# Gate columns from the raw input in plain fp32, 32 columns wide, on four column strips

## The chip, the cores and the metric

The kernel runs on one core of one Trainium2 chip. The metric is device time in microseconds (us). The kernel before takes 1498.56 us, the median of three runs (1497.97 to 1499.13).

## What is computed

One layer of a hybrid streaming trunk for 320 tokens (256 of a new stream, 64 of a running one), model width 2048. The part that matters here is the combined input projection, of whose columns the last 16 are the "gate columns" (8 for beta, 8 for the decay of the gated DeltaNet heads):

```python
h = rmsnorm(x, g_pre_mix)                  # x * rsqrt(mean(x*x) + eps) * g
p = h @ w_in
...
q, k, v, z, b_raw, a_raw = ...             # b_raw, a_raw: the 16 gate columns
beta = jax.nn.sigmoid(b_raw)
g = -jnp.exp(a_log) * jax.nn.softplus(a_raw + dt_bias)
o, s = gated_delta_chunked(q, k, v, hchunks(g), hchunks(beta), s0)
```

After it come a Conformer convolution over half of the mix width, the output projection, and a convolutional feed-forward network with the large w_up and w_down.

## The kernel before

Everything is held transposed: features on the 128 partitions, the 320 tokens along the free axis, so the width of 2048 is 16 k-blocks (KB). The row factor of RMSNorm (`rb`, a 128 x 320 tile that holds the same row of 320 numbers on every partition) is applied after the products, since it is one number for each token; the norm weight g1 is multiplied into the activations.

**Products.** Large products run in fp32r on values split in two: `whi` is the weight rounded by a ScalarE cast (L214), `wlo` the rest by a VectorE subtraction (L215), and the activations are split likewise (`hi_t`, `lo_t`, called hh and hl in the profile). Each 128 x 128 block of weights takes three matmuls of 128 x 320 (hi·hi L230, hi·lo L231, lo·hi L234). A projection block of 128 columns is 48 of them. Raw weights, `whi` and `wlo` have three buffers each; a projection block uses two (h1, h2: eight k-blocks each), so a cast waits for the matmuls that read the third-last `whi`.

**The order of the work.** The stream of these "dense" matmuls is written out block by block, and each is counted by `tick`. At every 20th tick the jobs that are due (generators: the norm, the gates, the stages of the DeltaNet, convolution taps) are advanced: their next piece of code is put behind the dense matmul that has just been issued, at a raised priority. Where a small job stands in each engine's queue thus hangs on the tick count.

**The start.** The first 192 matmuls make four blocks at once (`ps_first`, two z blocks, a q block and a k block) while the input arrives. Then come the gate columns, `gate_products` (L303): 32 dense matmuls from `hi_t` and `lo_t`, whose stationary operand `wbz` is 128 wide with the cast of the gate weights in columns 0 to 15, their rest in columns 16 to 31 and zeros beyond. They accumulate in the bank `psba`, of which 32 partitions are used. Then comes the block FIRST_V (number 48 of the projection, a v block), then block 25 and block 17 (k and q blocks), all in `psq` banks. The pool `ps_p` has two banks: psba, block 48, block 25 (in psba's bank) and block 17 (in block 48's) take them in turn, so block 17's first matmul waits until block 48's sum has been read, by `qb<-psq` (L623).

**The norm** is a job: `rstd` (six matmuls of one column, L256), then `rr` (DVE L261, POOL L262), and, 36 ticks later, `psb` (three transposes, L269) and `rb<-psb` (ACT L402). Behind `rb` wait, on VectorE, the two z tiles (L949), the q and k tiles `qb<-ps_first` (L623), the gates' `baT` (L424, L425) and the short convolution `cq` (L629, whose first tap is ACT L627), and then `qb<-psq`.

**The gates** are a job: `baT<-psba` (ACT L421, L422; 32 partitions), times `rb` (DVE L424, L425), three transposes of 32 x 128 (`pst_ba`, L430), a copy and an addition that sums the two halves (L432, L433), and small functions.

**The DeltaNet** runs pair by pair of heads in jobs beside the later projection blocks. Three places are named below: `px` (PE L789) waits for `zh` (ACT L784) in the inversion of small triangular blocks; `pvns` (PE L884) waits for `rhs` (DVE L876); and `pvn` (PE L855) for `rh` (DVE L896). Other VectorE work stands between these: the base inversion of the next pair (L745 to L759, 40 partitions), weight splits and convolution taps (L560).

Of the kernel before, what the change touches and what calls it, by code (L numbers as in the profile page):

```python
# [9 lines left out]
F32 = mybir.dt.float32  # L10
# [7 lines left out]
P = 128  # L18
D = 2048
KB = D // P  # L20
# [80 lines left out]
def trunk_kernel(ctx, tc, ins, outs):  # L101
# [46 lines left out]
    def tick(mm):  # L148
        dense[0] = mm.ins
        dense[1] += 1  # L150
        if dense[1] % GAP == 0:
            g, t0, behind, due = 0, held_t[0], dense[0], []
            t = t0
            n0 = len(nc.cur_bb.bb.instructions)
            for job in sorted(jobs, key=lambda j: j[0]):
                if job[0] <= dense[1] and g + job[2] <= 4 and t + job[3] <= 2:
                    g += job[2]
                    t += job[3]
                    due.append(job)
            for job in due:  # L160
                if not job[4]:
                    behind = advance(job, behind)
            scalar = newest(mybir.EngineType.Activation, n0)
            for job in due:
                if "scale" in job[4]:
                    with ExitStack() as e:
                        if scalar is not None:
                            e.enter_context(tc.issue_after(scalar))
                        advance(job)
            held_t[0] = t - t0  # L170
            front = newest(mybir.EngineType.DVE, n0)
            for _ in range(min(pace[0], len(taps))):
                next_tap(front)
# [21 lines left out]
    def cv(name, n=P, m=P):  # L195
        o, _ = CST[name]
        return cst[0:n, o:o + m] if o < NCST1 else cst2[0:n, o - NCST1:o - NCST1 + m]
# [106 lines left out]
    def gate_products(wz):  # L304
        psba = ps_p.tile([P, 512], F32, tag="p", name="psba")
        for k in range(KB):
            tick(PE.matmul(psba[:, 0:T], wz[:, k, :], hi_t[k], start=(k == 0), stop=False))
            tick(PE.matmul(psba[:, 0:T], wz[:, k, :], lo_t[k], start=False, stop=(k == KB - 1)))
        return psba


# [1 line left out]
    with tc.tile_pool(name="xp", bufs=1) as xp:  # L313
        xt = [xp.tile([P, 4, T], F32, tag=f"x{i}", name=f"xt{i}") for i in range(4)]
        wg = []

        def load_x(k0, k1):
            nc.sync.dma_start(xt[k0 // 4][:, k0 % 4:k0 % 4 + k1 - k0, :], ins["x"][:, k0:k1, :])

        def load_first(k0, k1):  # L320
            nc.sync.dma_start(wg[-1][:, (k0 % 2) * FW:(k0 % 2 + k1 - k0) * FW], ins["w_first"][:, k0 * FW:k1 * FW])

        with tc.high_priority():
            nc.scalar.dma_start(par[:, 0:NGV], ins["par"][:, 0:NGV])
            for k in range(0, KB, 2):
                wg.append(wst.tile([P, HALF], F32, tag="w", name="w"))
                for kk in ((k, k + 1), (k + 1, k + 2)) if k < 4 else ((k, k + 2),):
                    load_x(*kk)
                    load_first(*kk)
            nc.sync.dma_start(cst, ins["cst"][:, 0:NCST1])  # L330
            wba = xp.tile([P, KB, 16], F32, tag="wba", name="wba")
            nc.sync.dma_start(wba, ins["w_ba"])
        wbz = xp.tile([P, KB, P], F32R, tag="wbz", name="wbz")
        G.memset(wbz.bitcast(F32), 0.0)
        nc.sync.dma_start(par[:, NGV:NPAR], ins["par"][:, NGV:NPAR])
        nc.sync.dma_start(gpar[:, 0:8], ins["a_log"].partition_broadcast(P))
        nc.sync.dma_start(gpar[:, 8:16], ins["dt_bias"].partition_broadcast(P))
        psw = ps_g.tile([P, 512], F32, tag="g", name="psw")
        with tc.high_priority(offset=PRI_E):
            keep_warm(psw, NWARM)  # L340

            last = {}

            def then(eng, fn, *args, **kw):
                with ExitStack() as e:
                    if eng in last:
                        e.enter_context(tc.issue_after(last[eng].ins))
                    last[eng] = fn(*args, **kw)

            def split_part(hi, lo, w, o, n):  # L350
                then(S, S.copy, hi[:, o:o + n], w[:, o:o + n])
                then(V, V.tensor_tensor, lo[:, o:o + n], w[:, o:o + n], hi[:, o:o + n].bitcast(F32), ALU.subtract)

            ssum = xp.tile([P, 2, T], F32, tag="ssum", name="ssum")

            def squares(k):
                x = xt[k // 4][:, k % 4:k % 4 + 2, :]
                if k == 0:
                    then(S, S.activation, ssum, x, AF.Square)
                else:  # L360
                    sq = xp.tile([P, 2, T], F32, tag="sq", bufs=2, name="sq")
                    then(S, S.activation, sq, x, AF.Square)
                    then(V, V.tensor_tensor, ssum, ssum, sq, ALU.add)

            for k in range(KB):
                x = xt[k // 4][:, k % 4, :]
                g = pv("g1", k)
                then(S, S.activation, hi_t[k], x, AF.Identity, scale=g)
                then(V, V.scalar_tensor_tensor, lo_t[k], x, g, hi_t[k].bitcast(F32), ALU.mult, ALU.subtract)
                if k % 2 == 0:  # L370
                    pre.append((wsp.tile([P, HALF], F32R, tag="whi", name="whi"), wsp.tile([P, HALF], F32R, tag="wlo", name="wlo")))
                if k < 4:
                    split_part(*pre[-1], wg[k // 2], (k % 2) * FW, FW)
                elif k % 2:
                    split_part(*pre[-1], wg[k // 2], 0, 2 * FW)
                if k % 2 and k >= 5:
                    squares(k - 5)
            then(S, S.copy, wbz[:, :, 0:16], wba)
            then(V, V.tensor_tensor, wbz[:, :, 16:32], wba, wbz[:, :, 0:16].bitcast(F32), ALU.subtract)
            for k in (KB - 4, KB - 2):  # L380
                squares(k)
        for i, b in enumerate(FIRST):
            pool = (ps_t, ps_g)[i // 2]
            ready[b] = pool.tile([P, 512], F32, tag=pool.name[-1], name="ps_first")
        for k0 in range(0, KB, 2):
            hi, lo = pre[k0 // 2]
            for ks in ((k0,), (k0 + 1,)) if k0 < 4 else ((k0, k0 + 1),):
                for wt in (hi, lo):
                    for k in ks:
                        for i, b in enumerate(FIRST):  # L390
                            ps = ready[b][:, 0:T]
                            o = (k - k0) * FW + i * P
                            w = wt[:, o:o + P]
                            xh, xl = hx(k)
                            tick(PE.matmul(ps, w, xh, start=(k == 0 and wt is hi), stop=(k == KB - 1 and wt is lo)))  # L395
                            if wt is hi:
                                tick(PE.matmul(ps, w, xl, start=False, stop=False))

        def first_norm():
            rr, _ = rstd([ssum[:, 0, :], ssum[:, 1, :]])  # L400
            yield 36, 1, 0
            S.copy(rb, rstd_rows(rr)[0])  # L402

        job = start(first_norm(), 24, 1)
        psba = gate_products(wbz)
        ready[FIRST_V] = in_block(FIRST_V, "psq")
        finish(job)
# [5 lines left out]


    gate = {}
    cst2 = act.tile([P, NCST - NCST1], F32, tag="bl7", name="cst2")
    nc.sync.dma_start(cst2, ins["cst"][:, NCST1:NCST])

    def gates():
        baT = cb.tile([32, 3, P], F32, tag="un", bufs=1, name="baT").rearrange("p c f -> p (c f)")  # L420
        S.copy(baT[:, 0:T], psba[0:32, 0:T])  # L421
        S.copy(baT[:, T:T + TS], psba[0:32, TP:T])  # L422
        yield 1, 0, 0
        V.tensor_tensor(baT[:, 0:T], baT[:, 0:T], rb[0:32, :], ALU.mult)  # L424
        V.tensor_tensor(baT[:, T:T + TS], baT[:, T:T + TS], rb[0:32, TP:T], ALU.mult)  # L425
        ba = const.tile([P, 3, 16], F32, tag="ba", name="ba")
        yield LAG_WAIT, 0, 1
        pst = ps_t.tile([P, 512], F32, tag="t", name="pst_ba")
        for c in range(3):
            PE.transpose(pst[:, c * 32:(c + 1) * 32], baT[:, c * P:(c + 1) * P], cv("ident", 32, 32))  # L430
        ps3 = pst[:, 0:96].rearrange("p (c f) -> p c f", c=3)
        S.copy(ba, ps3[:, :, 0:16])  # L432
        V.tensor_tensor(ba, ba, ps3[:, :, 16:32], ALU.add)  # L433
        beta = const.tile([P, 3, NH], F32, tag="beta", name="beta")
        S.activation(beta, ba[:, :, 0:8], AF.Tanh, scale=0.5)
        G.tensor_scalar(beta, beta, 0.5, 0.5, ALU.mult, ALU.add)
# [878 lines left out]
```

## Time and profile before

| what | value |
|---|---|
| median of three runs | 1498.56 us (1497.97 to 1499.13) |
| the profiled execution's span, first to last instruction | 1497.8 us |
| mean granted TensorE clock in it | 0.997 |
| DVE busy | 996.1 us (67%) |
| ACT busy | 727.9 us (49%) |
| POOL busy | 229.2 us (15%) |
| DMA over the span | 149 GB/s |

The median stands 0.76 us above the span of the profiled execution; this covers what lies before the first and after the last instruction. PE is TensorE's matmuls, PEld its weight loads, DVE is VectorE, ACT ScalarE, POOL GpSimd, SP the engine that issues the DMAs. A busy time of the profile counts matmuls that overlap once. In a row of the timeline the columns are the start, the duration, the engine, the line, the operation and its tiles with their shapes, how many instructions the row holds, and in square brackets the idle time of that engine just before it and the instruction that ended it.

### The profile page before, as it was taken

Reading aid. Unit: us, or ns where it says so; the run is one execution under the profiler, and the core shown is the slowest. Engines: PE = TensorE matmul, PEld = TensorE weight load, DVE = VectorE, ACT = ScalarE, POOL = GpSimd, SP = SyncE. Lnnn points to the kernel's source line nnn. Section 1 sums busy time; section 2 is a strip of 40 time slices with the busy share of each in tenths; the row PEclk is TensorE's granted clock in tenths of the full one; section 3 lists DMA queues with packets and bytes.
Section 4 is the critical chain, followed back from the end, with each engine's and each line's share of the span. In section 5 each row is a group of like instructions: output and inputs, shape, how many; then the busy total and the mean of one; then the engine's idle time right before and its main releaser. Section 6 shows DMA issues by size and latency. Waiting matters only on the chain.

```text
span 1497.8 us, 27263 instructions
## 1 busy us (share of the span) xinstructions
PE 1481.6 (99%) x10609; PEld 1460.4 (98%) x10610; DVE 996.1 (67%) x1816; ACT 727.9 (49%) x1329; POOL 229.2 (15%) x390
## 2 busy tenths in 40 slices
PE   9999999999999999999999999999999999999998
PEld 8999999989999999999999999999999999999997
DVE  6779886978989678766345666445666545666554
ACT  7764556554544565544434444334444333444453
POOL 0111101120010000332002222002223101222101
PEclk9999999999999999999999999999999999999999
DMA  8435453544434744444554444455444455444453
GB/s 289 142 128 157 141 155 120 146 139 134 130 106 142 221 151 141 148 149 128 149 169 151 151 154 134 140 156 164 154 152 141 136 146 173 153 146 152 130 152 118
DMA packets 98281, 224.22 MB, mean 150 GB/s; under 512 B 18792, under 2 KB 39528, under 8 KB 98152
## 3 DMA queue, kind: packets, MB, share of 16 engines
q1 hardware_dynamic: 98008, 222.45, 47.7%
q8 instruction: 83, 1.36, 0.4%
q14 instruction: 46, 0.38, 0.1%
q10 hardware_dynamic: 144, 0.03, 0.0%
HBM read 215.33 MB, written 7.12 MB: 149 GB/s over the span
## 4 chain that ended last, share of the span: by engine, by line
PE 86%; DVE 6%; ACT 3%; DMA 2%; issue 2%; POOL 1%; SPq 0%; ACTq 0%; DVEq 0%
PE psu L234 13%; PE psu L231 13%; PE psu L230 13%; PE psdn L230 7%; PE psdn L231 6%; PE psdn L234 6%; PE psq L234 2%; PE psq L230 2%; PE psq L231 2%; PE psm L231 2%; PE psm L230 2%; PE psm L234 2%; DVE wlo L215 1%; PE psu L1108 1%; PE ps_first L395 1%
## 5 line engine op out<-in xcount | busy, mean ns | idle before, releaser
L214 ACT CAST whi<-w 128x1024 fp32r<-128x1024 f32 (+2 forms) x440 | 412.6, 940 | 481.7 <-PE psu L231 169.0
L215 DVE TENSOR_TENSOR wlo<-w,whi 128x1024 fp32r<-128x1024 f32 (+2 forms) x440 | 477.0, 1085 | 199.0 <-ACT whi L214 127.8
L230 PE MATMUL psu<-hi,whi 128*128 128x320 f32 x1344 | 397.0, 309 | 0.0
L231 PE MATMUL psu<-lo,whi 128*128 128x320 f32 x1344 | 397.0, 309 | 0.0
L230 PEld LDWEIGHTS psu<-hi,whi 128*128 128x128 f32 x1344 | 252.3, 188 | 0.0
L231 PEld LDWEIGHTS psu<-lo,whi 128*128 128x128 f32 x1344 | 252.3, 188 | 0.0
L234 PE MATMUL psu<-hi,wlo 128*128 128x320 f32 x1344 | 224.4, 309 | 0.0
L234 PEld LDWEIGHTS psu<-hi,wlo 128*128 128x128 f32 x1344 | 204.0, 188 | 0.0
L231 PE MATMUL psdn<-gl,whi 128*128 128x320 f32 x660 | 195.9, 310 | 0.0
L1141 POOL COPY nffn<-fbuf 128x2 f32<-128x2 f32 x88 | 101.5, 1153 | 586.9 <-DVE fbuf L1139 583.7
L1139 DVE TENSOR_TENSOR fbuf<-psu,rb 128x256 f32<-128x256 f32 x88 | 37.3, 424 | 168.9 <-PE psu L234 168.9
L230 PE MATMUL psdn<-gh,whi 128*128 128x320 f32 x480 | 142.8, 309 | 0.0
L231 PEld LDWEIGHTS psdn<-gl,whi 128*128 128x128 f32 x660 | 123.9, 188 | 0.3
L230 PE MATMUL psq<-hh,whi 128*128 128x320 f32 x352 | 106.2, 315 | 0.0
L231 PE MATMUL psq<-hl,whi 128*128 128x320 f32 x352 | 104.1, 309 | 0.0
L230 PEld LDWEIGHTS psdn<-gh,whi 128*128 128x128 f32 x480 | 90.1, 188 | 0.0
L234 PE MATMUL psdn<-gh,wlo 128*128 128x320 f32 x480 | 89.9, 309 | 0.0
L234 PEld LDWEIGHTS psdn<-gh,wlo 128*128 128x128 f32 x480 | 75.3, 188 | 0.0
L230 PEld LDWEIGHTS psq<-hh,whi 128*128 128x128 f32 x352 | 66.1, 188 | 0.3
L231 PEld LDWEIGHTS psq<-hl,whi 128*128 128x128 f32 x352 | 66.1, 188 | 0.2
L560 DVE SCALAR_TENSOR_TENSOR cvt<-ub,par,cvt 128x320 f32<-128x320 f32 x120 | 65.2, 543 | 0.2
L1184 DVE TENSOR_TENSOR y<-y,psdn 128x320 f32<-128x320 f32 x45 | 22.0, 488 | 59.1 <-PE psdn L234 59.1
(356 smaller groups left out, 2483.3 us busy)
## 6 DMA issues: line engine op xcount, KB each, us to landing
w<-in_w_up SPq DMA_DIRECT2D x176, 512.0 KB, 3.6
w<-in_w_in SPq DMA_DIRECT2D x88, 512.0 KB, 3.9
w<-in_w_down SPq DMA_DIRECT2D x64, 384.0 KB, 3.1
w<-in_w_down SPq DMA_DIRECT2D x64, 320.0 KB, 3.0
w<-in_w_out SPq DMA_DIRECT2D x32, 320.0 KB, 3.8
w<-in_w_out SPq DMA_DIRECT2D x16, 384.0 KB, 3.2
w<-in_w_first SPq DMA_DIRECT2D x6, 512.0 KB, 6.9
wtp<-wsp SPq DMA_DIRECT2D x4, 640.0 KB, 6.0
```

What stands on the lines that cost most here:

```text
L214: S.copy(hi[:, 0:width], w[:, 0:width])
L215: V.tensor_tensor(lo[:, 0:width], w[:, 0:width], hi[:, 0:width].bitcast(F32), ALU.subtract)
L230: tick(PE.matmul(ps, wh, xh, start=(first and k0 + j == 0), stop=False))
L231: tick(PE.matmul(ps, wh, xl, start=False, stop=False))
L234: tick(PE.matmul(ps, lo[:, j * P:(j + 1) * P], xh, start=False, stop=(final and k0 + j == nk - 1)))
L395: tick(PE.matmul(ps, w, xh, start=(k == 0 and wt is hi), stop=(k == KB - 1 and wt is lo)))
L560: return lambda: V.scalar_tensor_tensor(acc, x, w, acc, ALU.mult, ALU.add)
L1108: PE.matmul(pss[i][:, 0:T], wt[:, o:o + P], x, start=(k == 0 and n == 0), stop=(k == KB - 1 and n == 2))
L1139: V.tensor_tensor(buf[:, 2:258], psu[:, 0:TP], rb2[:, 0:TP], ALU.mult)
L1141: G.tensor_copy(nffn[:, b, 0, :], buf[:, 256:258])
L1184: V.tensor_tensor(y[:, n, :], y[:, n, :], psd[:, 0:T], ALU.add)
```

## The change

The gate columns are multiplied in plain fp32 from the raw input `xt`, 16 products of 128 x 32 (stationary) by 128 x 320 (moving). Product k writes the 32 output partitions from 32·(k mod 4), so that four products in a row use four different strips of 32 columns of the array, and psba holds four partial sums. The norm weight is multiplied into the 16 gate columns instead (DVE), `wbz` is 32 wide and its ScalarE cast goes; the memset that clears it covers 512 elements of a partition instead of 2048. The products are counted by 16 ticks, all behind the last one, where there were 32.

Behind them `baT` has 128 partitions instead of 32, and the three transposes become three plain fp32 products with `pick` (128 x 16: ones where partition mod 32 equals the column, made from the identity by a VectorE reduction), which sum the four strips and turn them at once. The addition of the two halves goes.

```diff
     def gate_products(wz):
         psba = ps_p.tile([P, 512], F32, tag="p", name="psba")
         for k in range(KB):
-            tick(PE.matmul(psba[:, 0:T], wz[:, k, :], hi_t[k], start=(k == 0), stop=False))
-            tick(PE.matmul(psba[:, 0:T], wz[:, k, :], lo_t[k], start=False, stop=(k == KB - 1)))
+            i = 32 * (k % 4)
+            mm = PE.matmul(psba[i:i + 32, 0:T], wz[:, k, :], xt[k // 4][:, k % 4, :], start=(k < 4), stop=(k >= KB - 4),
+                           skip_group_check=True)
+        for _ in range(16):
+            tick(mm)
         return psba
...
-        wbz = xp.tile([P, KB, P], F32R, tag="wbz", name="wbz")
-        G.memset(wbz.bitcast(F32), 0.0)
+        wbz = xp.tile([P, KB, 32], F32, tag="wbz", name="wbz")
+        G.memset(wbz, 0.0)
...
-            then(S, S.copy, wbz[:, :, 0:16], wba)
-            then(V, V.tensor_tensor, wbz[:, :, 16:32], wba, wbz[:, :, 0:16].bitcast(F32), ALU.subtract)
+            then(V, V.tensor_tensor, wbz[:, :, 0:16], wba, pv("g1").unsqueeze(2).to_broadcast((P, KB, 16)), ALU.mult)
...
+    pick = const.tile([P, 16], F32, tag="pick", name="pick")
...
     def gates():
-        baT = cb.tile([32, 3, P], F32, tag="un", bufs=1, name="baT").rearrange("p c f -> p (c f)")
-        S.copy(baT[:, 0:T], psba[0:32, 0:T])
-        S.copy(baT[:, T:T + TS], psba[0:32, TP:T])
+        baT = cb.tile([P, 3, P], F32, tag="un", bufs=1, name="baT").rearrange("p c f -> p (c f)")
+        S.copy(baT[:, 0:T], psba[:, 0:T])
+        S.copy(baT[:, T:T + TS], psba[:, TP:T])
+        V.tensor_reduce(pick, cv("ident").rearrange("p (a j) -> p j a", j=32)[:, 0:16, :], AX.X, ALU.add)
         yield 1, 0, 0
-        V.tensor_tensor(baT[:, 0:T], baT[:, 0:T], rb[0:32, :], ALU.mult)
-        V.tensor_tensor(baT[:, T:T + TS], baT[:, T:T + TS], rb[0:32, TP:T], ALU.mult)
+        V.tensor_tensor(baT[:, 0:T], baT[:, 0:T], rb, ALU.mult)
+        V.tensor_tensor(baT[:, T:T + TS], baT[:, T:T + TS], rb[:, TP:T], ALU.mult)
         ba = const.tile([P, 3, 16], F32, tag="ba", name="ba")
         yield LAG_WAIT, 0, 1
         pst = ps_t.tile([P, 512], F32, tag="t", name="pst_ba")
         for c in range(3):
-            PE.transpose(pst[:, c * 32:(c + 1) * 32], baT[:, c * P:(c + 1) * P], cv("ident", 32, 32))
-        ps3 = pst[:, 0:96].rearrange("p (c f) -> p c f", c=3)
-        S.copy(ba, ps3[:, :, 0:16])
-        V.tensor_tensor(ba, ba, ps3[:, :, 16:32], ALU.add)
+            PE.matmul(pst[:, c * 16:(c + 1) * 16], baT[:, c * P:(c + 1) * P], pick, start=True, stop=True)
+        S.copy(ba, pst[:, 0:48].rearrange("p (c f) -> p c f", c=3))
```

The lines of the changed program are numbered two to four higher than before. With 16 ticks fewer, the ticks at which jobs come due fall on other matmuls of the weight stream, and where a job's instructions stand on each engine shifts with them.

At the start of the program, on ScalarE, around the copy of `rb` from `psb`, there stood before (baT holds the gate columns, strict is a constant, whi is a weight cast, zT a z tile):

```order
L422 COPY baT<-psba 32x64
L471 CAST strict<-cst 128x128
L214 CAST whi<-w 128x1024
L402 COPY rb<-psb 128x320
L214 CAST whi<-w 128x1024
L950 ACT_TABLE_LOAD
L950 ACTIVATE zT_615<-zT_615 128x320
```

And now:

```order
L425 COPY baT<-psba 128x64
L473 CAST strict<-cst 128x128
L214 CAST whi<-w 128x1024 x3
L404 COPY rb<-psb 128x320
L952 ACT_TABLE_LOAD
L952 ACTIVATE zT_599<-zT_599 128x320
```

The casts ahead of the copy were those of block 25's second half; now those of block 17's two halves stand there too. On PE, `psb` stood behind 36 matmuls of `psq` (after all 32 gate products) and stands behind 64 now, while block 17 begins behind 96 in both.

On VectorE, around the two `rhs` of the third pair of heads (tmp, dn and wi are the base inversion of the pair after it, cvt and odd convolution taps, wlo a weight split, rh what pvn waits for, sg a gate tile of the convolution), there stood before:

```order
L752 TENSOR_TENSOR tmp<-dn,wi 40x512
L560 SCALAR_TENSOR_TENSOR odd<-ub_587,par,odd 128x320
L754 TENSOR_REDUCE dn<-tmp 40x64
L876 SCALAR_TENSOR_TENSOR rhs<-ks,neG,vh 64x128
L756 TENSOR_TENSOR tmp<-wi,dn 40x512
L533 TENSOR_TENSOR sg<-psgate,rb 128x320
L876 SCALAR_TENSOR_TENSOR rhs<-ks,neG,vh 64x128
```

And now:

```order
L878 SCALAR_TENSOR_TENSOR rhs<-ks,neG,vh 64x128
L747 TENSOR_TENSOR tmp<-wi,dn 40x72
L562 SCALAR_TENSOR_TENSOR cvt<-ub_571,par,cvt 128x320
L749 TENSOR_REDUCE wi<-tmp 40x2x6
L878 SCALAR_TENSOR_TENSOR rhs<-ks,neG,vh 64x128
L747 TENSOR_TENSOR tmp<-wi,dn 40x98
L239 TENSOR_TENSOR bl_4407<-af,bh_4406 128x320
L749 TENSOR_REDUCE wi<-tmp 40x2x7
L562 SCALAR_TENSOR_TENSOR odd<-ub_571,par,odd 128x320
L535 TENSOR_TENSOR sg<-psgate,rb 128x320
L754 TENSOR_TENSOR tmp<-dn,wi 40x512
L215 TENSOR_TENSOR wlo<-w,whi 128x1024
```

The wide steps of the base inversion (40x512) stood ahead of the two `rhs` and between them; now they stand behind both and ahead of `rh` (L898).

## The prediction

> **What bounds the kernel now.** I read the page first: the busy times, then the chain that ended last, with its shares by engine.
>
> ```profile
> PE 1481.6 (99%) x10609; PEld 1460.4 (98%) x10610; DVE 996.1 (67%) x1816; ACT 727.9 (49%) x1329; POOL 229.2 (15%) x390
> PE 86%; DVE 6%; ACT 3%; DMA 2%; issue 2%; POOL 1%; SPq 0%; ACTq 0%; DVEq 0%
> ```
>
> TensorE is busy for 1481.6 of 1497.8 us. So a matmul taken out shortens the kernel by its time, unless PE then waits; only some 16 us of waits exist. Next, the timeline of PE where it waits beside the DeltaNet, and the table of windows around two of these waits (in each engine's column the busy time; PEclk is the granted clock).
>
> ```profile
> 158.08 0.46 PE L789 MATMUL px<-wtp,zh 32*16 32x16 f32 x38 [0.97 <-ACT zh L784]
> 315.46 0.48 PE L789 MATMUL px<-wtp,zh 32*16 32x16 f32 x38 [1.95 <-ACT zh L784]
> 352.18 0.46 PE L884 MATMUL pvns<-rhs,wtp 128*128 128x128 f32 x2 [1.86 <-DVE rhs L876]
> core 0: us, PE busy (x) PEld busy (x) DVE busy (x) ACT busy (x) POOL busy (x), PEclk, DMA share, GB/s
> 312.00:316.00 4.00, 2.05 (x64) 1.78 (x65) 3.66 (x5) 2.97 (x8) 0.00 (x0) 0.94 0.58 198
> 316.00:320.00 4.00, 4.00 (x44) 3.96 (x39) 2.47 (x13) 1.35 (x6) 0.02 (x1) 0.63 0.45 137
> 350.00:354.00 4.00, 2.14 (x13) 1.98 (x13) 3.94 (x7) 2.61 (x10) 0.00 (x0) 0.89 0.08 10
> 354.00:358.00 4.00, 4.00 (x24) 4.00 (x23) 3.49 (x7) 1.23 (x3) 0.00 (x0) 0.69 0.58 145
> 159.00:163.00 4.00, 4.00 (x26) 3.87 (x27) 1.48 (x5) 3.43 (x11) 1.18 (x7) 1.00 0.31 105
> ```
>
> The waits of 1.95 and 1.86 us were each followed by a stretch at a lowered clock. From 312 to 320 the missing clock is 4·0.06 + 4·0.37 = 1.7 us of PE time, from 350 to 358 it is 4·0.11 + 4·0.31 = 1.7 us. After the wait of 0.97 us (the row 159 to 163) the clock stayed at 1.00. So a wait of PE near 2 us cost 1.7 us more than itself in both cases here.
>
> **The gate products.** PE's timeline has the first of them, its neighbours, the column sums of the norm that run among them, and the first matmul of block 48.
>
> ```profile
> 33.91 0.31 PE L307 MATMUL psba<-hh,wbz 128*128 128x320 f32 x1
> 38.02 1.40 PE L256 MATMUL pst<-cst,ssum 128*128 128x1 f32 x12
> 39.28 0.39 PE L307 MATMUL psba<-hh,wbz 128*128 128x320 f32 x1
> 39.96 0.31 PE L230 MATMUL psq<-hh,whi 128*128 128x320 f32 x1
> ```
>
> From 33.91 to 38.02 stand 28 products: 0.147 us each, 4.7 us for 32. The column sums took 1.26 us of PE (38.02 to 39.28), and stay. For a plain fp32 product of 128 x 128 by 128 x 320 the trace has the end of the program, which turns the output with one; for strips it has the small triangular blocks.
>
> ```profile
> 1487.13 2.33 PE L1230 MATMUL fin<-y,cst 128*128 128x320 f32 x8
> 1489.30 0.70 PE L1151 MATMUL fin<-x,cst 128*128 128x320 f32 x2
> 166.27 0.31 PE L231 MATMUL psz<-hl,whi 128*128 128x320 f32 x1
> 166.51 0.50 PE L806 MATMUL pz<-wtp,np 32*32 32x32 f32 x20
> 166.94 0.42 PE L230 MATMUL psz<-hh,whi 128*128 128x320 f32 x1
> 170.41 0.32 PE L815 MATMUL py<-zq,wtp 32*32 32x32 f32 x5
> ```
>
> The group of L806's records has their durations (least, median and most, in ns):
>
> ```profile
> L806 PEld LDWEIGHTS pz<-wtp,np x80: 101/108/108, 166.5 to 395.4; 32*32 32x32 f32 x80
> L806 PE MATMUL pz<-wtp,np x80: 191/191/212, 166.5 to 395.4; 32*32 32x32 f32 x80
> ```
>
> Eight records took 2.17 us, 0.271 each, and a plain fp32 product leaves two records (L806's ten products leave 20): 0.54 us a product, 8.7 us for 16 in series. So in plain fp32 the gates cost more, not less, unless the strips run beside each other. That they can: the L806 records, on two strips in turn, follow each other by (0.50 − 0.19)/19 = 16 ns, where those of L815, on one, take (0.32 − 0.19)/4 = 32 ns (0.19 us is one record's median). With four strips beside each other 16 products take four rounds of 0.54 us, 2.17 us, and going in and out of narrow tiles costs some 0.3 us (166.27 to 166.94 is 0.67 us for L806: less one dense product, 0.15, and 20 records of 16 ns, 0.2 are left, and the wider last record is still running). I take **G = 2.45 us** for the gates; the bound above is 8.7 (no overlap), the bound below 2.2. Saved on PE: 4.7 − 2.45 = 2.25 us.
>
> [...] In the trace L815 and its neighbour L813 share rows and interleave, but only with 32 rows; the case of 128 rows is in no row here. [...]
>
> **What waits next.** The products are not followed by a stream that is always ready: block 17 needs the bank of block 48, which VectorE frees behind `rb`. ScalarE's, VectorE's and PE's timelines have that chain:
>
> ```profile
> 45.23 0.49 PE L269 MATMUL psb<-cst,rr 128*128 128x128 f32 x3
> 45.76 0.43 ACT L402 COPY rb<-psb 128x320 f32<-128x320 f32 x1 [2.21 <-PE psb L269]
> 46.22 0.89 DVE L949 TENSOR_TENSOR zT<-ps_first,rb 128x320 f32<-128x320 f32 x2 [1.26 <-ACT rb L402]
> 46.35 1.05 ACT L214 CAST whi<-w 128x1024 fp32r<-128x1024 f32 x1 [0.16 <-PE psq L231]
> 47.42 1.28 ACT L950 ACT_TABLE_LOAD   x1
> 48.35 1.21 DVE L215 TENSOR_TENSOR wlo<-w,whi 128x1024 fp32r<-128x1024 f32 x1
> 50.33 2.87 DVE L629 SCALAR_TENSOR_TENSOR cq<-qb,par,cq 128x320 f32<-128x320 f32 x6 [0.77 <-ACT cq L627]
> 53.11 0.48 DVE L623 TENSOR_TENSOR qb<-psq,rb 128x320 f32<-128x320 f32 x1
> 53.68 1.33 PE L234 MATMUL psq<-hh,wlo 128*128 128x320 f32 x8
> 54.86 0.31 PE L230 MATMUL psq<-hh,whi 128*128 128x320 f32 x1
> 51.52 0.37 PE L430 MATMUL pst_ba<-cst,baT 32*128 32x32 f32 x3
> ```
>
> The bank was free at 53.59, and PE came to block 17 at 54.86: 1.27 us of slack, less than what the gates save. And `psb` moves: by the order it stands behind 64 matmuls of psq, not 36.
>
> After the change, in the times of this trace: gates to 33.91 + 2.45 = 36.36; 12 matmuls, 38.1; column sums, 39.4; 52 matmuls, 47.0; `psb` ends at 47.5. Ahead of the copy ScalarE now has the cast of block 17's second half, which may start only when block 25's first half has been read, just ahead of `psb`: 47.2 to 48.2. The copy of `rb` ends at 48.65, where it ended at 46.19. From there to the end of `qb<-psq` it took 7.40 us; the wait of 0.77 goes, as ScalarE now loads its table right behind the copy, so 6.63, and the bank is free at **55.3**. PE gets there at 47.0 + 0.25 for psb (half of its 0.49 lies beside the next matmul) + 32·0.147 + 0.8 for the gates' three fp32 products (an estimate: the three transposes took 0.37 in one place, and these stand in two) = 52.8. It idles for 2.5 us, and block 17 starts at 55.3 where it started at 54.86: **+0.45 us**. The whole saving becomes a wait. In general block 17 starts at 52.85 + G, so the early part gains only if G is under 2.0.
>
> A wait of 2.5 us is longer than both that were followed by a lowered clock. I take 1.7 us with a chance of 0.7: **+1.2 us**, bounds 0 and 1.7. [...]
>
> Other edits of this stage: one cast of 256 elements leaves ScalarE; the VectorE multiply replaces a subtraction of the same size; one addition of 0.2 us goes and `pick` comes, all before or beside PE's 192 first matmuls or in the shadow of the wait. Copies and products of `baT` on 128 partitions have the same free size, so I take the old durations. POOL's shorter memset hides nothing. I cost them at 0, at most 0.3 us either way.
>
> **Later stages.** The jobs stand elsewhere in the stream. By the order `zh` still follows the activations of the v tile that delayed it, so the wait at 315 stays. The two `rhs` now stand ahead of the wide steps of the base inversion; the timelines of VectorE and PE show what those cost, and when `ks` and `pvn` run:
>
> ```profile
> 347.88 1.05 DVE L752 TENSOR_TENSOR tmp<-dn,wi 40x512 f32<-40x512 f32 x1
> 349.33 0.67 DVE L754 TENSOR_REDUCE dn<-tmp 40x64 f32<-40x512 f32 x1
> 350.18 1.06 DVE L756 TENSOR_TENSOR tmp<-wi,dn 40x512 f32<-40x512 f32 x1
> 345.47 1.03 PE L872 MATMUL ks<-s,kqs 128*128 128x256 f32 x4
> 361.43 0.60 PE L855 MATMUL pvn<-rh,wtp 128*128 128x128 f32 x4
> ```
>
> Without 1.05 + 0.67 + 1.06 in front, `rhs` is ready some 2.8 us sooner and the wait of 1.86 us with its 1.7 us of clock goes: −3.6 us. But between the second `rhs` and `rh` (L898) now lie, by the order, 14 instructions of VectorE: the four wide steps (two of 1.05, two of 0.67, taken alike), two weight splits of 1.21 and eight smaller ones at some 0.4, 9 us in all. PE asked for `rh` 14.9 us after `ks` ended (346.5 to 361.43), 11.3 without the 3.6, and `rhs` takes its part of that. A wait of 0 to 3 us can arise at `pvn` (PE L855); I take 1.6, and 0.8 for the clock behind it (1.7 at even odds). Together **−1.2 us**, bounds −3.6 and +1.2.
>
> Sum on the execution's own 1497.8: +0.45 + 1.2 − 1.2 = +0.45, 1498.25 in span; with the 0.76 us by which the median stands above it, **1499.0 us**.
>
> **The rivals.**
> - *Saving kept in part.* `rb` is copied as soon as `psb` ends (47.5), the cast of block 17 having run before. The chain then ends at 54.5, block 17 starts 0.4 us earlier than before, and the wait of 1.7 us is too short for the clock: 1498.56 − 0.4 − 1.2 = 1497.0. Against it: the cast stands ahead of the copy in ScalarE's order, and PE frees its buffer only just ahead of psb. Chance 0.1.
> - *The later wait goes for good.* `rh` is in time: 1498.56 + 0.45 + 1.2 − 3.6 = 1496.6, and 1495.4 without the early lowered clock. For it: 9 us of VectorE against 11.3. Chance 0.25.
> - *Strips that overlap badly*, the slower side. Half overlap gives G = 4.6 and block 17 at 57.45, +2.6; with 1.2 of clock and −1.2 later, 1501.2. No overlap gives G = 8.7, +6.7, 1505.3. It passes +0.2% (3 us) from G = 5.0. For it: 128 rows are shared, and no row here shows four such products. Against it: L806 and L815. Chance 0.17.
> - [...] Chance 0.03.
>
> **How the numbers follow.** The forecast, 1499.0 (own range 1496.5 to 1502), has 0.45. About 0.2% or 3.0 us, so 1495.6 to 1501.6, is what a measurement of this kernel can tell from no change. Faster holds the part of the later-wait rival without lowered clock and the lower ends of the first rival and the forecast: 0.18. Slower holds the strips above G = 5.0, the series and the forecast's upper end (a wait at `pvn` of 3 us with its clock): 0.22. The rest, 0.60, lies within. The range of 8 in 10 runs from 1495.0 (early clock kept, `rh` in time) to 1504.0 (strips a little better than without overlap).
>
> **What would show it.** The gates' first record to the last some 2.2 us apart; `rb` copied near 48.6; an idle time of PE near 2.5 us at block 17's first matmul, put down to `qb<-psq`, and a granted clock under 0.9 in the 4 us after it; no wait at `pvns` of the third pair, and one at `pvn` or none. Wrong would be: the records of psba 0.27 us apart in series; no wait at block 17; a new wait in a place that isn't named here, such as DMA.

## The result, and the profile after

The changed kernel takes 1503.49 us, the median of four runs (1502.39 to 1505.37), beside 1498.26 for the kernel before: a ratio of 1.0037, with a 95% interval of 1.0024 to 1.0049. Six more runs, made later with other kernels, have a median of 1503.26 (ratio 1.0028, 1.0016 to 1.0040). It is slower by some 5 us (the medians are 5.2 and 4.9 apart). The profiled execution has a span of 1500.6 us; the device time stands 1.8 us above the span in every run of it, so this was the fastest of the four (1502.39). The 0.76 us by which the median of before stands above the span of its trace is therefore not the time outside the first and last instruction: that trace, 1497.8 in span, is of an execution that took longer than most, and the later runs of the kernel before have spans around 1496.4. So the two traces are 2.8 us apart where the medians are 5.

The page after, its busy times and its chain:

```profile
PE 1482.4 (99%) x10613; PEld 1457.6 (97%) x10613; DVE 997.4 (66%) x1816; ACT 728.5 (49%) x1328; POOL 227.0 (15%) x390
PE 84%; DVE 7%; ACT 3%; DMA 2%; issue 2%; POOL 2%; DVEq 0%; ACTq 0%; POOLq 0%
```

TensorE holds 84% of the chain instead of 86%; VectorE and GpSimd, which it waits for, hold 1% more each. PE's timeline at the start, with the casts and copies of ScalarE and the chain on VectorE behind them:

```profile
34.12 2.36 PE L308 MATMUL psba<-xt,wbz 128*32 128x320 f32 x32
38.27 1.39 PE L256 MATMUL pst<-cst,ssum 128*128 128x1 f32 x12
47.23 0.49 PE L269 MATMUL psb<-cst,rr 128*128 128x128 f32 x3
47.43 1.05 ACT L214 CAST whi<-w 128x1024 fp32r<-128x1024 f32 x1 [1.68 <-PE psq L231]
48.39 0.42 ACT L404 COPY rb<-psb 128x320 f32<-128x320 f32 x1
52.11 2.86 DVE L631 SCALAR_TENSOR_TENSOR cq<-qb,par,cq 128x320 f32<-128x320 f32 x6
54.89 0.88 DVE L625 TENSOR_TENSOR qb<-psq,rb 128x320 f32<-128x320 f32 x2
55.52 0.39 PE L230 MATMUL psq<-hh,whi 128*128 128x320 f32 x1 [2.42 <-DVE qb L625]
```

The gates took 2.36 us. `rb` was copied at 48.39, behind the cast, and PE waited 2.42 us at block 17. (The v block called number 48 further up is number 32 of the projection; 48 is its count of matmuls. Nothing was worked out from the name.)

Further on, the waits of PE from 30 to 400 us, first of before, then of after (line, what it waited for, us in total, times, longest):

```profile
PE px L789 <- ACT zh L784: 2.9, 2, 2.0
PE pvns L884 <- DVE rhs L876: 1.9, 1, 1.9
PE px L813 <- ACT zq L808: 0.6, 1, 0.6
PE psg L476 <- DVE gt L459: 0.3, 1, 0.3
```

```profile
PE psq L230 <- DVE qb L625: 2.4, 1, 2.4
PE px L791 <- ACT zh L786: 2.2, 2, 1.7
PE px L815 <- ACT zq L810: 1.7, 2, 1.1
PE pvn L857 <- DVE rh L898: 0.9, 1, 0.9
PE pks L712 <- ACT vh L704: 0.8, 1, 0.8
PE pk L708 <- ACT vh L704: 0.3, 1, 0.3
PE psg L478 <- DVE gt L461: 0.2, 1, 0.2
```

The wait at `pvns` is gone and a smaller one at `pvn` has come. But `pks` (products of keys of the first pair of heads, called pair 0 here) now waits for `vh`, and `px` for `zq` in pair 0's inversion. The table of windows has the granted clock behind the wait at block 17 (first row) and around the `zq` waits:

```profile
56.00:60.00 4.00, 4.00 (x30) 4.00 (x29) 4.00 (x9) 2.81 (x10) 0.00 (x0) 1.00 0.40 132
172.00:176.00 4.00, 2.35 (x37) 1.97 (x36) 3.57 (x12) 2.61 (x7) 1.20 (x2) 1.00 0.38 131
176.00:180.00 4.00, 4.00 (x29) 3.96 (x22) 3.90 (x12) 1.46 (x4) 0.00 (x0) 0.58 0.48 175
```

The two waits (1.11 and 0.55 us, close together) were followed by 1.7 us of lost clock (4 us at 0.58 of the full clock), where the wait of 2.42 us at block 17 was followed by none in this execution.

### The profile page after: what moved, and what is told of

Same layout as the page of the kernel before. It is cut to its first block, busy times and chain, and to the rows that moved or that the text cites. A ratio compares the mean times of both kernels' runs of the same rounds, so it can differ in the third digit from the quotient of the medians.

```text
span 1500.6 us, 27267 instructions
## 1 busy us (share of the span) xinstructions
PE 1482.4 (99%) x10613; PEld 1457.6 (97%) x10613; DVE 997.4 (66%) x1816; ACT 728.5 (49%) x1328; POOL 227.0 (15%) x390
## 4 chain that ended last, share of the span: by engine, by line
PE 84%; DVE 7%; ACT 3%; DMA 2%; issue 2%; POOL 2%; DVEq 0%; ACTq 0%; POOLq 0%
PE psu L234 13%; PE psu L230 13%; PE psu L231 13%; PE psdn L230 7%; PE psdn L231 6%; PE psdn L234 6%; DVE wlo L215 2%; PE psq L230 2%; PE psq L231 2%; PE psq L234 2%; PE psu L1110 1%; PE psm L234 1%; PE psm L230 1%; PE psm L231 1%; PE ps_first L397 1%
```

## The experiments

I took the time from one large matmul to the next, in each trace, and subtracted that of before, for stretches of the program that lie between jobs. Matmuls are counted from the first of the 192 at the start; the gate products are not counted. The table has the stretches in which the kernels differ most. Left out are the start up to 48, where the input arrives, the stretch from 1160 to 1855 (0.3 to 1.2 us shorter than before in all six) and the last one that waits for weights, from 2700 to 2950, which moves by 1 to 2 us from one execution to another. In us:

| stretch (matmuls) | after | before_ticks16 | rb_early | late16 | ticks32 | rb_ticks32 |
|---|---|---|---|---|---|---|
| 48 to 290: gates, norm, to block 17 | +0.63 | +2.73 | −2.10 | +0.52 | +0.94 | −2.14 |
| 290 to 535: the gates' functions | −0.15 | +1.74 | +0.52 | −0.15 | +1.78 | +0.58 |
| 535 to 640: pair 0, pk and pks | +1.05 | +1.05 | +1.05 | −0.01 | −0.02 | −0.01 |
| 780 to 1160: pair 0, inversion and chain | +3.07 | +2.97 | +4.11 | −0.20 | −0.31 | −0.06 |
| 1855 to 2030: pair 2, rhs and rh | −2.23 | −1.96 | −2.27 | −1.63 | −1.85 | −2.13 |

Every column differs from the same one trace of before, which lost clock twice, 1.7 us behind each of its waits near 2 us; the second of these losses lies in the last row (behind `pvns`). That row is negative in all six columns for this reason, also in late16 and ticks32, whose wait at `pvns` stayed.

The first three experiments set three theories against each other; the places of a job are where its instructions stand in the queues. **Theory 1**: most of the loss comes from the places that the later jobs got when 16 ticks went. **Theory 2**: it comes from the start, the wait at block 17 and what follows it. **Theory 3**: the new products themselves cost it.

**ticks32.** The changed kernel with the gates counted as before.

```diff
-        for _ in range(16):
+        for _ in range(32):
             tick(mm)
```

> The changed kernel with its gate products counted by 32 ticks, as before, so that every later job stands where it stood before; the start (2.36 us of gate products, psb behind 64 of block 48's and 25's matmuls by way of the casts, a wait of some 2.4 us at block 17) is meant to stay. Theory 1 (the jobs' new places cost most of the 5.2 us): block 17 starts 0.4 us later than before, with a lowered clock of 0 to 1.7 us behind the wait, and nothing else: 1498.7 to 1500.4 us. Theory 2 (the wait at block 17 and what follows it cost all of it): as the changed kernel, 1503.5 us.

1495.75 us, median of 12 (ratio to before 0.9985, 0.9977 to 0.9993): faster than both kernels, and faster than either theory had it. The later jobs cost nothing more than before, as the table's last rows show. I had assumed that the start would stay as in the changed kernel, and it did not: PE met the late `rb` at the gates' three small products, as the timelines show.

```profile
45.58 0.49 PE L269 MATMUL psb<-cst,rr 128*128 128x128 f32 x3
46.51 1.05 ACT L214 CAST whi<-w 128x1024 fp32r<-128x1024 f32 x1 [2.57 <-DMA w<-in_w_in]
47.46 0.42 ACT L404 COPY rb<-psb 128x320 f32<-128x320 f32 x1
50.86 0.62 PE L434 MATMUL pst_ba<-pick,baT 128*128 128x16 f32 x4 [1.27 <-DVE baT L428]
53.92 0.48 DVE L625 TENSOR_TENSOR qb<-psq,rb 128x320 f32<-128x320 f32 x1
```

`psb` stands behind 52 matmuls here, `rb` comes 1 us sooner, and the bank of block 17 is free at 54.40 instead of 55.37. The wait is 1.27 us, half as long. (This profiled execution lost clock behind it, 0.97 and 0.61 of the full clock in the 8 us from 48, and again at 72 us, 0.57 for 4 us, behind a wait of 0.54 us at `psg`, 3.4 us together, more than the +0.94 and +1.78 in its column; it was the slowest of the 12.) So this run bears on the places, and not on how much the start costs.

**before_ticks16.** The kernel before, in which only one of each two gate products is counted.

```diff
-            tick(PE.matmul(psba[:, 0:T], wz[:, k, :], hi_t[k], start=(k == 0), stop=False))
+            PE.matmul(psba[:, 0:T], wz[:, k, :], hi_t[k], start=(k == 0), stop=False)
```

> The kernel before with only one of each two gate products counted, 16 ticks; the products themselves stay as before. The jobs then stand as in the changed kernel. Theory 1: the places cost as much as there, and the gates take 2.25 us more than there: 1505.7 us, and the trace has the changed kernel's later waits (pks, zq, pvn). Theory 2: only the start costs, block 17 at 57.5 us instead of 54.9, with a lowered clock of 0 to 1.7 us: 1501 to 1502.7 us. If the strips or the wider products cost it (theory 3), then 1498.3 us.

1504.9 us (ratio 1.0040, 1.0028 to 1.0052). With none of the new products, it has the changed kernel's loss and its waits (PE's, from 30 to 400 us):

```profile
PE psq L230 <- DVE qb L623: 2.3, 1, 2.3
PE px L813 <- ACT zq L808: 1.6, 2, 1.1
PE pvn L855 <- DVE rh L896: 0.9, 1, 0.9
PE pks L710 <- ACT vh L702: 0.8, 1, 0.8
```

Theory 3 falls: 16 ticks less, by themselves, cost the kernel before 6.8 us; less the 2.2 us that the new products save, that is about the changed kernel's loss. Taking the tick count away moves both the start and the places, so theories 1 and 2 needed the next three kernels.

**rb_early.** The changed kernel, with `psb` issued 28 ticks sooner and the large matmuls behind it held behind it, so that the scheduler cannot put them ahead.

```diff
-            yield 36, 1, 0
-            S.copy(rb, rstd_rows(rr)[0])
+            yield 8, 1, 0
+            row, mm = rstd_rows(rr)
+            ahead.append(mm.ins)
+            S.copy(rb, row)
...
-                tick(PE.matmul(ps, wh, xh, start=(first and k0 + j == 0), stop=False))
+                with ExitStack() as e:
+                    if ahead and dense[1] < 400:
+                        e.enter_context(tc.issue_after(ahead[0]))
+                    mm = PE.matmul(ps, wh, xh, start=(first and k0 + j == 0), stop=False)
+                tick(mm)
```

> The changed kernel with psb behind 32 matmuls of psq and held there, so that the chain from rb to the bank of block 17 starts some 5 us sooner; the later jobs stay where the change put them. The wait at block 17 should be gone in either theory. Theory 1: 2.4 us less than the changed kernel, and up to 1.7 us of clock: 1499.4 to 1501.1 us. Theory 2: the whole of the 5.2 us goes and the saving of 2.2 us stays: 1496 us.

1499.08 us, median of 11 (ratio 1.0009, 0.9999 to 1.0019). `rb` is copied at 43.51, the bank that block 17 takes is free at 50.45, and the wait at block 17 is gone. The later waits of PE stay:

```profile
PE px L822 <- ACT zq L817: 2.8, 2, 2.2
PE px L798 <- ACT zh L793: 2.3, 2, 1.8
PE pvn L864 <- DVE rh L905: 0.9, 1, 0.9
PE psg L485 <- DVE gt L468: 0.8, 1, 0.8
PE pks L719 <- ACT vh L711: 0.8, 1, 0.8
```

**rb_ticks32.** The same, with 32 ticks (`yield 24` in place of 8), so that start and places are both cured.

> Both: psb behind 36 matmuls and held there, and 32 ticks. Theory 1 and theory 2: no wait at block 17, later jobs as before, the gates' saving stays: 1496.1 us, 2.2 us under the kernel before. Rival: later waits (for weight casts or for zh and rhs, which hang on ScalarE and VectorE) take the saving up, and it is 1498.3 us.

1496.51 us, median of 12 (ratio 0.9994, 0.9983 to 1.0004). By the medians, 1.6 of the 2.2 us that the gates save show, though the interval just holds no change; PE waits 0.9 us at `psg`, a product of the gates' functions, where it waited 0.3 us before.

**late16.** The fourth corner: the start as the change made it, the places as before.

```diff
     def tick(mm):
+        count(mm)
+        if dense[1] == 508 and not late:
+            late.append(1)
+            for _ in range(16):
+                count(mm)
...
+    def count(mm):
```

> The changed kernel, and 16 ticks more at the 300th matmul behind the first 192, in block 17: the start stays as the change made it (psb behind 64, the wait of 2.4 us at block 17), the jobs behind it stand as before the change. With the changed kernel (1503.5), rb_early (1499.1) and rb_ticks32 (1496.5) this is the fourth corner of a square of start and places. If start and places add up: 1503.5 - 2.6 = 1500.9 us. If the places cost nothing by themselves and only follow from the late start: 1503.5 us. If the places are all: 1498.3 us or less.

1500.25 us, median of 11 (ratio 1.0013, 1.0005 to 1.0022). The 16 ticks come behind matmul 492, at 89 us in its trace. That is in the fourth block behind block 17, not in block 17 itself as the expectation has it, but ahead of pair 0's `pk` and `pks`; up to there its stretches are those of the changed kernel (+0.52 and −0.15). The wait at block 17 is there, and the waits at `pks`, `zq` and `pvn` are replaced by that of before, at `pvns` (PE's longest waits by line):

```profile
PE px L800 <- ACT zh L795: 3.0, 3, 1.8
PE psq L239 <- DVE qb L634: 2.4, 1, 2.4
PE pvns L895 <- DVE rhs L887: 1.8, 1, 1.8
```

The square, medians in us (the changed kernel's from all of its ten runs; the kernel before: 1498.1 to 1498.4):

| | jobs' places of the change | jobs' places of before |
|---|---|---|
| start of the change | 1503.4 | 1500.25 |
| rb early | 1499.08 | 1496.51 |

The start costs 4.3 us with the one set of places and 3.7 with the other; the places cost 3.2 and 2.6. The two add up to within 0.6 us, which is less than the scatter of the runs. So neither theory was right alone: the start takes back all that the gates save and 2 us more (late16 beside the kernel before), the places add 3.

**series.** The same gate products, but four in a row write one strip.

```diff
-            i = 32 * (k % 4)
+            i = 32 * (k // 4)
... (start and stop of the sums moved to the first and last product of a strip)
```

> The changed kernel with the strip changing after every four products instead of at every product, so four in a row write the same 32 partitions; the same products otherwise. If strips must alternate in the queue to run beside each other: 16 times 0.54 us, 8.7 us from the first record of psba to the last instead of 2.36, and block 17 some 6 us later. If TensorE reaches further down its queue: 2.4 to 4 us.

One execution, 1505.88 us, and for the gates, on PE's timeline:

```profile
34.01 5.66 PE L308 MATMUL psba<-xt,wbz 128*32 128x320 f32 x32
```

5.66 us, between the two. The records show how: on one strip they follow each other by 0.269 us, and the first product of the next strip starts 1.11 us after that of the strip before, just behind the fifth of that one's eight records. The program has the four products of a strip before those of the next, so three records of the strip before start later than a product that stands behind them: TensorE took products from further down, but only some way.

**ticks24.** 24 ticks instead of 16.

> The changed kernel with 24 ticks for the gates; the later jobs stand 8 matmuls from where they stood before (psb behind 56). If the later waits hang on the exact place: a value of its own between 1495.8 (32 ticks) and 1503.5 us (16 ticks), with waits at other places than in either. If the cost grows with the distance from the old places: half way, 1498 to 1500 us.

1502.29 us, median of 8 (ratio 1.0026, 1.0016 to 1.0036). It has almost no wait at block 17 (0.3 us) and loses its time at places where none of the others does, or not so long, as PE's waits show:

```profile
PE px L791 <- ACT zh L786: 5.8, 2, 4.2
PE pks L712 <- ACT vh L704: 1.6, 1, 1.6
PE psq L234 <- DVE wlo L215: 1.4, 1, 1.4
PE pz L824 <- ACT wtp L818: 1.3, 1, 1.3
```

Half way back to the old places, the time isn't half way back (1498 to 1500 us): the waits hang on the exact order, not on the distance alone.

**warm** and **late16_warm.** The changed kernel, and late16, with nine products of zeros in the wait at block 17. Block 17's matmuls are held behind them, as large matmuls are in rb_early.

```diff
+        if b == 17:
+            pw = ps_t.tile([P, 512], F32, tag="t", name="pw")
+            with tc.issue_after(dense[0]):
+                for _ in range(9):
+                    ahead[0] = PE.matmul(pw, wz[:, 0:P], wz, start=True, stop=True)
```

> The changed kernel with nine products of zeros (128 x 512, bf16) ahead of block 17's first matmul, in a bank of their own, so that TensorE has something to do in most of the wait of 2.4 us; nothing waits for them. If the wait costs a lowered clock behind it in some of the executions: 0.5 to 1.7 us less than the changed kernel, 1501.8 to 1503.0, with a mean granted clock higher by 0.0004 to 0.001 (0.9968 in the changed kernel's four). If the clock is lowered by the later waits alone: 1503.5 us and the same clock. If the nine products last longer than the wait: more than 1503.5.

> late16 (the start of the change, the places of before; 1500.25 us, mean clock 0.9978) with nine products of zeros in the wait at block 17. If the wait there has a lowered clock behind it in part of the executions: 0.5 to 1.5 us less than late16, 1498.8 to 1499.8 us, and a mean clock near that of the kernel before (0.9987). If not: 1500.25 us and 0.9978.

> The changed kernel once more, beside kernels on one chip and with more runs than its first four: 1503.5 us, 1502 to 1505. What is wanted is its mean granted clock beside that of the next kernel; the first four gave 0.9968.

warm: 1502.85 us, median of 5, mean clock 0.9978. The changed kernel again: 1503.26, 0.9963 (its four before: 0.9968). late16_warm: 1499.87, median of 12, clock 0.9990; late16 had 1500.25 and 0.9978. The row of the zeros and the rest of the wait, in late16_warm:

```profile
53.16 2.12 PE L319 MATMUL pw<-wz 128*128 128x512 bf16 x9
55.75 0.39 PE L243 MATMUL psq<-hh,whi 128*128 128x320 f32 x1 [0.47 <-DVE qb L645]
```

The clock came back: in late16_warm to that of before (0.9988 over 29 runs), in warm a good half of the way. Neither trace has a lowered clock behind block 17 (1.00 from 48 to 80 us in both). But the time fell by only 0.4 to 0.6 us, less than the clock would give (for late16 an estimate of 1.8 us, 0.0012 of 1500), and the runs of each pair overlap (late16 1497.99 to 1502.15, late16_warm 1498.55 to 1503.58). The traces show where some of it went: both kernels with zeros have a wait that the others lack, at `tv`, a transposition of v (PE's waits from 30 to 400 us, first of warm, then of late16_warm):

```profile
PE tv L691 <- ACT vT L644: 1.3, 1, 1.3
PE tv L700 <- ACT vT L653: 1.2, 1, 1.2
```

From matmul 1160 to 1855, where these waits lie, warm is 1.3 us longer than changed_again and late16_warm 2.3 us longer than late16. So the zeros changed more than the clock; why `vT` comes later with them was not followed. That the wait at block 17 has a lowered clock behind it in part of the executions is shown; what this costs in the median isn't settled by these runs. The trace of the changed kernel run again has it, at once behind the wait (PE's timeline, and the table of windows):

```profile
55.59 0.39 PE L230 MATMUL psq<-hh,whi 128*128 128x320 f32 x1 [2.43 <-DVE qb L625]
56.00:60.00 4.00, 4.00 (x19) 4.00 (x18) 3.93 (x8) 1.72 (x5) 0.00 (x0) 0.59 0.38 132
```

## Why the prediction was right, and where it was wrong

The time fell inside the range, but not where the likeliest case had it. 1499.0 was forecast as no change, and the kernel is slower. That the range holds the time is luck: its upper end, 1504.0, was drawn for strips that hardly overlap, and the strips overlap fully.

**The gates: right.** G was put at 2.45 us and is 2.36. In plain fp32, four strips beside each other, each strip's records follow by 0.269 us (forecast 0.271 from the output's products). The 32 loads of 0.11 us, 3.5 us if one followed the other, start between 34.1 and 35.8 us and lie beside the matmuls, which start between 34.1 and 36.0, although all four strips use all 128 rows. The chance of 0.22 for slower counts 0.03 for loads in series with the products. No run shows such loads: the trace has the 16 products with their loads in 2.36 us.

**The start: right, both parts.** `rb` was forecast at 48.65 to end, and ended at 48.81; the bank free at 55.3, and PE went on at 55.52; the wait of 2.5 us was 2.42; block 17 began 0.66 us later than before (55.52 and 54.86), of which 0.21 is a later start of the gates in this execution (34.12 and 33.91): +0.45, as forecast. The lowered clock behind the wait was taken as 1.7 us with a chance of 0.7: of the five traces with a wait of this length (after, changed_again, before_ticks16, series, late16) three have it (in windows of 4 us from 56 us: 0.59 in changed_again, 0.79 and 0.79 in before_ticks16, 0.76, 0.50 and 0.89 in series; 1.00 in after and late16). Together, +1.65 was forecast; late16, which has this start and the places of before, is 2 us slower than the kernel before. Waits of 0.54 to 2.43 us had a lowered clock behind them in some traces; the one longer wait, 4.2 us in ticks24, had one too (0.82, 0.50 and 0.83 in the 12 us from 316). The first rival's step that a wait of 1.7 us is too short for it is not borne out: 1.69 us at `zh` in the first trace after the change had 0.57 behind it (320 to 324 us), while 1.9 us at the same place in ticks32 had 1.00. The copies and products of `baT`, taken at their old durations, took 417, 206, 483 and 218 ns on 128 partitions, and 416, 198, 471 and 206 on 32.

**Later stages: wrong.** The step that failed is the term of −1.2 us ("Together −1.2 us, bounds −3.6 and +1.2"). The waits that it worked out came about: the wait at `pvns` went (0 us in this trace; up to 1.2 is left in later ones), a wait at `pvn` came (0.93; I took 1.6), the one at `zh` stayed (1.69; 1.95 before). What the vanished wait is worth was put too high: the term counts 1.7 us of clock behind it as lost in every execution, because the one trace of before has it. In late16, ticks32 and rb_ticks32 the wait at `pvns` stayed (1.8, 1.5 and 1.3 us), with a clock of 1.00 behind it in all three (348 to 364 us), and yet the stretch around it takes 1.6 to 2.1 us less than in that trace; the changed kernel takes 2.2 us less. So the new places gain at most some 0.6 us there. And the term took the rest of the later jobs to be as before, and only two places had been looked at. The change from late16 to the changed kernel measures the whole: +3.2 us instead of −1.2. It sits in pair 0 (+1.05 at `pks`, and +3.07 around `zq`, of which 1.7 is lost clock). The order there has changed as well. ScalarE's timeline after the change:

```profile
173.31 1.16 ACT L590 ACTIVATE un<-pt_c,gnm,grs 128x128 f32<-128x128 f32 x3 [3.82 <-POOL gnm L586]
174.49 0.28 ACT L810 COPY zq<-pz 32x160 f32<-32x160 f32 x1
174.80 0.47 ACT L952 ACTIVATE zT<-zT 128x320 f32<-128x320 f32 x1
175.28 0.28 ACT L810 COPY zq<-pz 32x160 f32<-32x160 f32 x1
```

The two halves of `zq` stand behind `un`, a piece of the convolution, that waits 3.8 us for POOL, and one z tile stands between them. Before, `zq` also stood behind `un`, as the timelines of ScalarE and PE in the trace of before have it:

```profile
168.24 1.16 ACT L588 ACTIVATE un<-pt_c,gnm,grs 128x128 f32<-128x128 f32 x3 [2.73 <-POOL gnm L584]
169.42 0.60 ACT L808 COPY zq<-pz 32x160 f32<-32x160 f32 x2
170.07 0.41 PE L813 MATMUL px<-wtp,zq 32*32 32x32 f32 x14
```

PE came to `px` just as both halves had been copied (169.42 and 0.60, 170.02; `px` at 170.07). There was no slack in that place to lose, and no wait in the profile of before to point at it. What made POOL's part later against PE, and `vh` later at `pks`, was not followed; that it goes with the places is what late16 shows.

**The rivals.** Strips that overlap badly did not come about. The saving was not kept in part. That the later wait goes for good was half right (`pvns`), and given back elsewhere. The slower side was foreseen only as a price of the strips; the mechanism that made the kernel slower was none of the rivals. That the change works, where its jobs stand as before, was not foreseen either: ticks32, at 1495.75 us, is the best version that I ran, 2.3 us under the kernel before (1.0 to 3.4 by its interval), about what the gates save.

## What to carry to other kernels

Where a counter of the main stream paces the side jobs, replacing n instructions by fewer must keep the count, or every later job moves; here that cost 3 us in waits and the clock behind them, more than the 2.2 us that the products save, and one number (32 for 16) turned a loss of 5 us into a gain of 2.3. When a change moves the jobs, compare the order at every place where TensorE waits for a small result, not only at the waits that the profile of before shows: a place without a wait may have no slack. And what is saved ahead of a chain that TensorE will meet later is worth only that chain's slack (1.27 us here) unless the chain's start moves with it.

## What the runs showed of the hardware

Four plain fp32 products of 128 x 32 on four column strips, with all 128 rows in use, run fully beside each other when they alternate in the queue (2.36 us for 16); with four in a row on one strip it is 5.66 us: there a strip's first product starts 1.11 us after that of the strip before, behind the fifth of that one's eight records. A lowered clock that costs some 1.7 us (3.4 in series, and in ticks24 behind 4.2 us) follows waits of 0.54 us (0.57 of the full clock, in ticks32) to 2.43 us in some executions of one program and not in others: the wait at block 17 is 2.42 and 2.43 us in two traces of the changed kernel, with the clock at 1.00 behind the one and 0.59 behind the other. This is a part of the scatter between runs: the changed kernel's ten lie between 1500.55 and 1506.07 us, with a mean clock of 0.996 to 0.998 in the five shortest and 0.995 or 0.996 in the five longest, and 0.001 of clock is an estimated 1.5 us (0.001 of 1500). Other waits differ between executions too (2.2 us at `zq` in changed_again, 1.1 and 0.5 in the first trace).
